# Gates of a recurrent branch: full 128-row matmuls with zero blocks, or two 64-row matmuls side by side

## The chip, the cores and the metric

One core of one Trainium2 chip runs the whole kernel as one launch. The time is device microseconds (us) of that core. TensorE (PE) multiplies matrices and writes to PSUM, ScalarE (ACT) evaluates functions, VectorE (DVE) does elementwise work, GpSimd (POOL) some small work, and SyncE (SP) issues the DMAs.

## The reference

An encoder trunk of two layers on 512 tokens of width 1024. In each layer one projection of the normalised input feeds four mixers, whose outputs are gated, projected, merged and added. The branch at stake is B, a recurrent unit on 384 channels in 6 blocks of 64, run forward and backward:

```python
xb = xc.reshape(b, s, B_BLOCKS, B_BLOCK_DIM)          # 6 blocks of 64
r = sigmoid(einsum("bsnc,ncd->bsnd", xb, w_r).reshape(b, s, w) + b_r)
i = sigmoid(einsum("bsnc,ncd->bsnd", xb, w_i).reshape(b, s, w) + b_i)
log_a = -B_C * r * softplus(-lam)
a = exp(log_a)
u = sqrt(-expm1(2.0 * log_a)) * (i * xc)
h = associative_scan(h[t] = a[t] * h[t-1] + u[t])     # per direction, the two are summed
```

Here xc is the output of a short depthwise convolution. The two gates r and i of a block are 64 x 64 matrices applied to that block's 64 channels.

## The kernel before, in words

Activations lie with channels on the 128 partitions and the 512 tokens along the free dimension. Every fp32 operand is split into a high and a low part of type fp32r, and a product is three matmuls, high x high, high x low and low x high (`mm3`, line 435). The low part is a subtraction on DVE, the high part a copy on ACT (`split`, line 427).

Three streams of work are generators: the dense stream (projections, gates, output), a side stream that runs the attention branches D, C and A one after another, and the recurrent branch (`side_B`, line 1290). `drive` (line 1854) asks them for their next steps and interleaves them. A planner (`Sched`, line 96) holds a clock for each engine and prices each instruction; it issues PE's instructions at once and holds those of the other engines back until they are due. Its price for a matmul of type fp32r with 256 or more columns goes by the columns alone (line 188), so 64 rows cost as much as 128. What comes out is one fixed order of instructions for each engine.

A stream tells through its yields what it waits for: `("c", n)` ends a step, `("w", label)` waits for another stream, `("n", k)` for free slots, and `self.at(..., S=1)` for operands and for that many free PSUM banks of pool S. Pool S has two banks (`BANKS`, line 46), and the scores of the attention branches use the same pool: D takes one bank at a time, C two. The recurrent branch is paced by its count of steps: between `B_FROM` and `B_TO` of the dense stream's cost in a layer it should make `B_STEPS` of them (line 54, used in `behind`, line 1902).

For each layer, `side_B` issues the DMAs of the gate weights into three zeroed tiles, one for each chunk of 128 channels, which is two blocks. Both blocks stand on the diagonal of a 128 x 128 matrix, one matrix for each direction and gate, and the other two quarters are zero. For each chunk it then computes the convolution on DVE, splits it into xh and xl, and for each direction and gate runs one trio of matmuls into one bank of pool S, followed by one tanh on ACT that reads the bank. Further ACT and DVE work and a scan on DVE follow. The result is handed over under the label yb, for which the dense stream waits (`split_y`, line 760) right behind the projection of a_v, which is 384 columns wide.

Branch C's scores already use halves of the rows. This is the form that they have (line 1431):

```python
for x, y in ((0, 0), (0, 1), (1, 0)):
    for c in range(2):
        r = slice(64 * c, 64 * c + 64)
        PE.matmul(Sb[c], (qh, ql)[x][r, s], (kh, kl)[y][r], start=(x == 0 and y == 0), stop=(x == 1))
```

The biases and other small parameters are loaded as rows, one per 128 channels, and turned once at the start, so that each becomes a column of the tile prm (`ROWS`, line 37; `load_params`, line 1739; `par`, line 1732).

Of the kernel before, what the change touches and what calls it, by code (L numbers as in the profile page):

```python
# [12 lines left out]
AF = mybir.ActivationFunctionType  # L13
# [3 lines left out]
P = 128  # L17
# [7 lines left out]
for _n, _s in IN_SPLITS:  # L25
# [8 lines left out]

K_C, K_A1, K_A23, K_RT, K_RN, K_QS, K_END = 0, 896, 1280, 1536, 2048, 2304, 2436

ROWS = {"b_gate": (0, 32), "conv_w": (64, 12), "conv_b": (88, 3), "lru_br": (94, 6), "lru_bi": (106, 6),
        "lru_lambda": (128, 6), "diff_subln": (140, 1), "mla_q_norm": (142, 2), "mla_kv_norm": (146, 1)}

P_QN, P_SUB, P_HSP, P_NSP, P_LAM = 0, 4, 6, 18, 30  # L40
# [10 lines left out]
SIDE_RESERVE = 9  # L51
LAYER_COST = 2670.0
PACE = ((80, 0), (940, 230), (1720, 430), (2290, 582))
B_FROM, B_TO, B_STEPS = 170, 560, 70
AHEAD = 0.1
AHEAD_OF = {"A": 0.7, "V": 0.7, "G": 0.7, "D": 100.0}
DELTA = {"s": 0.0, "d": 1.5, "w": 1.5, "b": 10.0}
# [306 lines left out]
class Trunk:  # L364
# [925 lines left out]
    def side_B(self, l):  # L1290
        nc, I = self.nc, self.I
        V, S = nc.vector, nc.scalar
        yield ("w", ((l, "hT"), 3))
        yield ("n", 3)
        raws = []
        for i in range(3):
            t = self.slot("lru")
            nc.gpsimd.memset(t, 0.0)
            v = t.rearrange("p (d w e) -> p d w e", d=2, w=2)
            for wi, wn in enumerate(("lru_wr", "lru_wi")):  # L1300
                src = I[wn][l].rearrange("d n c e -> n c d e")
                for o in range(2):
                    nc.sync.dma_start(v[64 * o:64 * o + 64, :, wi, 64 * o:64 * o + 64], src[2 * i + o])
            raws.append(t)
        yield ("w", (l, "bx"))
        for i in range(3):
            yield ("n", 9)
            wh, wl = self.slot("lruh", F32R), self.slot("lrul", F32R)
            self.split(wh, wl, raws[i])
            self.rel(raws[i])  # L1310
            bx = self.T.pop(f"bx{i}")
            xc = self.slot("xc")
            cw = lambda j: self.par("conv_w", l, 3 * j + i)
            V.tensor_scalar(xc, bx, cw(1), self.par("conv_b", l, i), op0=OP.mult, op1=OP.add)
            yield ("c", 0)
            V.scalar_tensor_tensor(xc[:, 1:], bx[:, :511], cw(0), xc[:, 1:], op0=OP.mult, op1=OP.add)
            yield ("c", 0)
            V.scalar_tensor_tensor(xc[:, :511], bx[:, 1:], cw(2), xc[:, :511], op0=OP.mult, op1=OP.add)
            yield ("c", 0)
            V.scalar_tensor_tensor(xc[:, :510], bx[:, 2:], cw(3), xc[:, :510], op0=OP.mult, op1=OP.add)  # L1320
            self.rel(bx)
            yield ("c", 0)
            xh, xl = self.slot("xch", F32R), self.slot("xcl", F32R)
            self.split(xh, xl, xc)
            yield ("c", 0)
            D = []
            for d in range(2):
                pr = []
                for wi, row in ((0, "lru_br"), (1, "lru_bi")):
                    yield self.at(wl, xl, S=1)  # L1330
                    B = self.ps("S")
                    c = slice((2 * d + wi) * P, (2 * d + wi) * P + P)
                    self.mm3(B, wh[:, c], wl[:, c], xh, xl, True, True)
                    t = self.slot("lg")
                    S.activation(t, B, AF.Tanh, scale=0.5, bias=self.par(row, l, 3 * d + i, self.prm_h))
                    pr.append(t)
                    yield ("c", 3)
                tr, ti = pr
                a = self.slot("la")
                k = 6 * l + 3 * d + i  # L1340
                hsp, nsp = self.der(P_HSP + k), self.der(P_NSP + k)

                S.activation(a, tr, AF.Exp, scale=nsp, bias=nsp)
                S.activation(tr, tr, AF.Tanh, scale=hsp, bias=hsp)
                yield ("c", 0)
                V.scalar_tensor_tensor(a, a, 1.0, tr, op0=OP.add, op1=OP.mult)
                V.tensor_scalar(a, a, -1.0, 1.0, op0=OP.mult, op1=OP.add)
                yield ("c", 0)
                V.scalar_tensor_tensor(ti, ti, 1.0, xc, op0=OP.add, op1=OP.mult)
                yield ("c", 0)  # L1350
                V.scalar_tensor_tensor(ti, a, 1.0, ti, op0=OP.add, op1=OP.mult)
                D.append((a, tr, ti))
                yield ("c", 0)
            self.rel(wh, wl, xh, xl, xc)
            for a, w, ti in D:
                S.activation(w, w, AF.Sqrt, scale=0.25, bias=self.tiny)
            for d, (a, w, ti) in enumerate(D):
                V.tensor_mul(ti, ti, w)
                yield ("c", 0)
                if d == 0:  # L1360
                    V.tensor_tensor_scan(w, a, ti, 0.0, op0=OP.mult, op1=OP.add)
                else:
                    V.tensor_tensor_scan(w[:, ::-1], a[:, ::-1], ti[:, ::-1], 0.0, op0=OP.mult, op1=OP.add)
                self.rel(a, ti)
                yield ("c", 0)
            if i == 0:
                yield ("w", (l, "ub"))
            u, w0, w1 = self.T.pop(f"ub{i}"), D[0][1], D[1][1]
            V.tensor_add(w0, w0, w1)
            yield ("c", 0)  # L1370
            V.tensor_mul(u, u, w0)
            self.rel(w0, w1)
            self.y_done("b", i, u, (l, "yb") if i == 2 else None)
            yield ("c", 0)
# [357 lines left out]
    def par(self, name, l, i, tile=None):  # L1732
        c = ROWS[name][0] + ROWS[name][1] * l + i
        return (self.prm if tile is None else tile)[:, c:c + 1]
# [4 lines left out]
    def load_params(self):  # L1739
        nc, I = self.nc, self.I  # L1740
        rows, lam = self.slot("rows"), self.slot("lam")
        nc.gpsimd.memset(rows[:, :256], 0.0)
        for name, (r, n) in ROWS.items():
            ap = I[name]
            c = P * (r // P)
            r, n = r % P, n * DEPTH
            nc.sync.dma_start(rows[r:r + n, c:c + P], bass.AP(tensor=ap.tensor, offset=ap.offset, ap=[[P, n], [1, P]]))
        v = lam.rearrange("p (i l c) -> p i l c", i=4, l=DEPTH)
        for i, n in enumerate(("diff_lam_q1", "diff_lam_k1", "diff_lam_q2", "diff_lam_k2")):
            s = I[n]  # L1750
            nc.sync.dma_start(v[:, i], bass.AP(tensor=s.tensor, offset=s.offset, ap=[[0, P], [64, DEPTH], [1, 64]]))
        self.rows = (rows, lam)

    def params(self):
# [8 lines left out]
        V.tensor_copy(self.prm, T[:, :256])  # L1763
        col = lambda n: self.prm[:, ROWS[n][0]:ROWS[n][0] + ROWS[n][1] * DEPTH]

# [220 lines left out]
```

## Time and profile before

| what | value |
|---|---|
| median of 3 runs | 1549.57 us (1548.51 to 1549.97) |
| the profiled execution's own time | 1549.14 us |
| its span, first to last instruction | 1547.4 us |
| busy PE / DVE / ACT / POOL | 1532.6 / 882.4 / 735.3 / 61.0 us |
| instructions | 21989 |
| mean granted TensorE clock | 0.996 |

Matmuls overlap: one lasts about 0.39 us in the records, and the next may start 0.23 us after it. So in a timeline the distance between two starts is what a matmul takes of PE. All instructions carry line 315, that of the planner's helper, so the tiles tell them apart: xch and xcl are the two parts of the convolution's output, lruh and lrul those of the gate weights, lg the gates, ck and cq the keys and queries of branch C, yb the branch's output.

### The profile page before, as it was taken

The page shows a single profiled execution, that of the slowest core. Times are in us where ns is not written, and L with a number is a line of the kernel's source. Part 1 is how long each engine was busy: PE and PEld are TensorE (multiplying, and loading weights), DVE is VectorE, ACT ScalarE, POOL GpSimd, SP SyncE. Part 2 cuts the span into 40 slices and gives each one's busy share as a digit, 9 for nine tenths or more (in the row PEclk, how much of TensorE's full clock was granted, in tenths as well). Part 3 has the DMA queues.
Part 4 walks back from the last instruction along what each step waited for, and adds up shares of the span by engine and source line. Part 5 has one row for each costly group of instructions (what it writes and reads, how often), then busy time and mean ns, then how long its engine had stood idle before and what let it go on. Part 6 is the DMA issues. An engine that isn't in the chain of part 4 may idle for free.

```text
span 1547.4 us, 21989 instructions
## 1 busy us (share of the span) xinstructions
PE 1532.6 (99%) x8024; PEld 1254.7 (81%) x8024; DVE 882.4 (57%) x1898; ACT 735.3 (48%) x1626; POOL 61.0 (4%) x254
## 2 busy tenths in 40 slices
PE   8999999999999999999999999999999999999998
PEld 8888888788887888888888878887787887788886
DVE  5698755446544453556658876544546446445553
ACT  5676653343444543443457765434435445334331
POOL 1300000000000100000020000000000001000000
PEclk9999999999999999999999999999999999999999
DMA  6422132223232324253252222232232223332621
GB/s 210 143 58 58 45 103 79 79 72 96 69 81 70 87 75 108 59 175 108 73 165 55 69 55 77 81 87 66 79 97 62 77 74 86 81 96 59 186 70 55
DMA packets 170884, 136.34 MB, mean 88 GB/s; under 512 B 25230, under 2 KB 158360, under 8 KB 170648
## 3 DMA queue, kind: packets, MB, share of 16 engines
q1 hardware_dynamic: 170776, 134.94, 31.3%
q8 instruction: 63, 1.03, 0.3%
q14 instruction: 45, 0.37, 0.1%
HBM read 129.45 MB, written 4.27 MB: 86 GB/s over the span
## 4 chain that ended last, share of the span: by engine, by line
PE 96%; DVE 1%; ACT 1%; DMA 0%; issue 0%; SPq 0%; DVEq 0%; ACTq 0%
PE ps L315 96%; DMA st<-in_w_in 0%; ACT lg L315 0%; DVE wl L315 0%; DVE lg L315 0%; DVE hTl L315 0%; ACT hTh L315 0%; ACT wh L315 0%; DVE rr L315 0%; SPq L315 0%; DVE rp L315 0%; ACT h L315 0%; ACT L315 0%; DVE x L315 0%; ACT la L315 0%
## 5 line engine op out<-in xcount | busy, mean ns | idle before, releaser
L315 PE MATMUL ps<-hTh,wh 128*128 128x512 f32 x1280 | 515.8, 403 | 1.1 <-DVE ud L315 1.1
L315 PE MATMUL ps<-hTl,wh 128*128 128x512 f32 x1280 | 499.7, 390 | 0.0
L315 PE MATMUL ps<-hTh,wl 128*128 128x512 f32 x1280 | 499.5, 390 | 0.0
L315 DVE TENSOR_TENSOR wl<-st,wh 128x512 fp32r<-128x512 f32 (+2 forms) x464 | 301.6, 666 | 272.0 <-ACT wh L315 271.1
L315 PEld LDWEIGHTS ps<-hTh,wh 128*128 128x128 f32 x1280 | 240.4, 188 | 62.8 <-issue 12.8
L315 ACT ACTIVATE wh<-st 128x512 fp32r<-128x512 f32 (+2 forms) x464 | 265.5, 606 | 42.2 <-DMA st<-in_w_in 35.9
L315 PEld LDWEIGHTS ps<-hTh,wl 128*128 128x128 f32 x1280 | 240.3, 188 | 52.2
L315 PEld LDWEIGHTS ps<-hTl,wh 128*128 128x128 f32 x1280 | 240.8, 188 | 44.5
L315 DVE CUSTOM_DVE_ANT_0 pC<-ps,cst 128x512 f32<-128x512 f32 x64 | 41.6, 689 | 81.5 <-PE ps L315 81.5
L315 PE MATMUL ps<-wh,hTh 128*128 128x416 f32 (+2 forms) x192 | 71.6, 373 | 0.6 <-ACT hTh L315 0.6
L315 PE MATMUL ps<-wl,hTh 128*128 128x416 f32 (+2 forms) x192 | 70.2, 365 | 1.7 <-DVE wl L315 1.6
L315 PE MATMUL ps<-wh,hTl 128*128 128x416 f32 (+2 forms) x192 | 69.9, 364 | 0.1
L315 ACT ACTIVATE pA<-pA,on 128x256 f32<-128x256 f32 x96 | 47.9, 501 | 38.1 <-DVE on L315 37.9
L315 ACT ACTIVATE pD<-ps,mx 128x512 f32<-128x512 f32 x48 | 33.0, 687 | 65.9 <-DVE mx L315 65.7
L315 ACT ACTIVATE pC<-pC,mx 128x512 f32<-128x512 f32 x64 | 45.8, 717 | 36.2 <-DVE mx L315 36.2
L315 DVE CUSTOM_DVE_ANT_0 pA<-ps,cst 128x256 f32<-128x256 f32 x96 | 36.0, 420 | 31.5 <-PE ps L315 31.4
L315 PE MATMUL ps<-wh,mh 128*128 128x512 f32 x128 | 50.0, 390 | 0.0
L315 PE MATMUL ps<-wh,ml 128*128 128x512 f32 x128 | 49.8, 389 | 0.0
L315 PE MATMUL ps<-wl,mh 128*128 128x512 f32 x128 | 49.8, 389 | 0.0
L315 ACT ACTIVATE wtC<-ps 128x512 f32<-128x512 f32 x32 | 19.1, 596 | 50.5 <-PE ps L315 50.5
L315 ACT ACTIVATE junk<-ps,rd 128x128 f32<-128x128 f32 x32 | 11.7, 365 | 63.8 <-DVE oC L315 63.1
L315 PEld LDWEIGHTS ps<-wl,hTh 128*128 128x128 f32 x192 | 36.6, 191 | 5.9 <-DVE wl L315 2.8
(390 smaller groups left out, 2207.8 us busy)
## 6 DMA issues: line engine op xcount, KB each, us to landing
st<-in_w_in SPq DMA_DIRECT2D x216, 256.0 KB
st<-in_w_in SPq DMA_DIRECT2D x240, 128.0 KB
st<-in_w_out SPq DMA_DIRECT2D x32, 256.0 KB
x<-in_x SPq DMA_DIRECT2D x16, 256.0 KB
st<-in_w_br_c SPq DMA_DIRECT2D x16, 256.0 KB
x<-x SPq DMA_DIRECT2D x16, 256.0 KB
st<-in_w_in SPq DMA_DIRECT2D x16, 208.0 KB
st<-in_w_in SPq DMA_DIRECT2D x16, 192.0 KB
```

Of the source, the lines that this page charges most:

```text
L315: op.fn(*op.a, **op.k)
```

## The change

The two gates of a block now stand side by side in the 128 columns of the stationary operand, and the two blocks of a chunk in the two halves of the rows. A group of six matmuls, each on 64 rows, gives both gates of both blocks for one direction, in two banks: bank o holds block o, its partitions 0 to 63 the first gate, 64 to 127 the second. Four tanh on 64 partitions each read them, and write the gates in the layout as before, so what follows is unchanged. The gate tiles are 256 columns wide, without zeros and without the memset. The biases of the two gates are loaded side by side in one row per block, so that one column holds both.

```diff
-B_FROM, B_TO, B_STEPS = 170, 560, 70
+B_FROM, B_TO, B_STEPS = 170, 560, 64
...
             t = self.slot("lru")
-            nc.gpsimd.memset(t, 0.0)
-            v = t.rearrange("p (d w e) -> p d w e", d=2, w=2)
+            v = t[:, :256].rearrange("p (d w e) -> p d w e", d=2, w=2)
...
-                    nc.sync.dma_start(v[64 * o:64 * o + 64, :, wi, 64 * o:64 * o + 64], src[2 * i + o])
+                    nc.sync.dma_start(v[64 * o:64 * o + 64, :, wi, :], src[2 * i + o])
...
-            self.split(wh, wl, raws[i])
+            self.split(wh[:, :256], wl[:, :256], raws[i][:, :256])
...
-                pr = []
-                for wi, row in ((0, "lru_br"), (1, "lru_bi")):
-                    yield self.at(wl, xl, S=1)
-                    B = self.ps("S")
-                    c = slice((2 * d + wi) * P, (2 * d + wi) * P + P)
-                    self.mm3(B, wh[:, c], wl[:, c], xh, xl, True, True)
-                    t = self.slot("lg")
-                    S.activation(t, B, AF.Tanh, scale=0.5, bias=self.par(row, l, 3 * d + i, self.prm_h))
-                    pr.append(t)
-                    yield ("c", 3)
-                tr, ti = pr
+                yield self.at(wl, xl, S=2)
+                B = [self.ps("S"), self.ps("S")]
+                c = slice(d * P, d * P + P)
+                for x, y in ((wh, xh), (wh, xl), (wl, xh)):
+                    for o in range(2):
+                        r = slice(64 * o, 64 * o + 64)
+                        self.PE.matmul(B[o], x[r, c], y[r], start=(x is wh and y is xh), stop=(x is wl))
+                tr, ti = self.slot("lg"), self.slot("lg")
+                for o in range(2):
+                    for g, t in enumerate((tr, ti)):
+                        r = slice(64 * g, 64 * g + 64)
+                        S.activation(t[64 * o:64 * o + 64], B[o][r], AF.Tanh, scale=0.5,
+                                     bias=self.par("lru_b", l, 6 * d + 2 * i + o, self.prm_h)[r])
+                yield ("c", 4)
...
+            if name == "lru_b":
+                for i, m in enumerate(("lru_br", "lru_bi")):
+                    ap = I[m]
+                    nc.sync.dma_start(rows[r:r + n, c + 64 * i:c + 64 * i + 64],
+                                      bass.AP(tensor=ap.tensor, offset=ap.offset, ap=[[64, n], [1, 64]]))
+                continue
```

## Rows read from the trace of the kernel before

**Rows 1.** Engine shares: busy us (share of the span) x instructions

```profile
PE 1532.6 (99%) x8024; PEld 1254.7 (81%) x8024; DVE 882.4 (57%) x1898; ACT 735.3 (48%) x1626; POOL 61.0 (4%) x254
```

**Rows 2.** The chain that ended last, by engine

```profile
PE 96%; DVE 1%; ACT 1%; DMA 0%; issue 0%; SPq 0%; DVEq 0%; ACTq 0%
```

**Rows 3.** Waits of PE: waited for, us in total, times, longest

```profile
PE ps L315 <- DVE h L315: 2.8, 3, 1.2
PE ps L315 <- DVE wl L315: 1.6, 2, 1.0
PE ps L315 <- DVE ud L315: 1.1, 1, 1.1
PE ps L315 <- DVE z L315: 1.1, 1, 1.1
PE ps L315 <- ACT hTh L315: 0.6, 1, 0.6
```

**Rows 4.** Timeline of PE, both gates of one direction: start, duration, instruction

```profile
77.73 0.39 PE L315 MATMUL ps<-xch,lruh 128*128 128x512 f32 x1
77.96 0.39 PE L315 MATMUL ps<-xcl,lruh 128*128 128x512 f32 x1
...
79.09 0.39 PE L315 MATMUL ps<-wh,hTh 128*128 128x512 f32 x1
```

**Rows 5.** Groups of instructions by form, PE: count, busy us, mean ns

```profile
L315 PE MATMUL ps<-xch,lruh 128*128 128x512 f32 x24 | 9.6, 402 | 0.0
```

**Rows 6.** Timeline of PE, the stretched trio

```profile
153.32 0.40 PE L315 MATMUL ps<-xch,lruh 128*128 128x512 f32 x1
153.75 0.50 PE L315 MATMUL ps<-xcl,lruh 128*128 128x512 f32 x1
154.09 0.39 PE L315 MATMUL ps<-xch,lrul 128*128 128x512 f32 x1
```

**Rows 7.** Timeline of PE, a group of branch C and its neighbours

```profile
299.52 0.39 PE L315 MATMUL ps<-hTh,wl 128*128 128x512 f32 x1
299.84 0.50 PE L315 MATMUL ps<-ck0h,cq0h 64*128 64x512 f32 x2
300.17 0.40 PE L315 MATMUL ps<-ck0l,cq0h 64*128 64x512 f32 x2
300.41 0.40 PE L315 MATMUL ps<-ck0h,cq0l 64*128 64x512 f32 x2
300.73 0.50 PE L315 MATMUL ps<-hTh,wh 128*128 128x512 f32 x1
301.07 0.40 PE L315 MATMUL ps<-hTl,wh 128*128 128x512 f32 x1
```

**Rows 8.** Groups of instructions by form, ACT

```profile
L315 ACT ACTIVATE lg<-ps,prmh 128x512 f32<-128x512 f32 x24 | 16.2, 682 | 6.1 <-PE ps L315 5.9
...
L315 ACT ACTIVATE lruh<-lru 128x512 fp32r<-128x512 f32 x6 | 3.7, 618 | 0.0
L315 ACT ACTIVATE ktd<-ps 64x512 f32<-64x512 f32 x6 | 3.6, 596 | 1.1 <-DVE ktl L315 1.0
```

**Rows 9.** Timeline of ACT, two tanh end to end

```profile
79.57 1.24 ACT L315 ACTIVATE lg<-ps,prmh 128x512 f32<-128x512 f32 x2
```

**Rows 10.** Busy time by stretch: busy us (x instructions), PEclk, DMA share, GB/s

```profile
80.00:175.00 95.00, 94.85 (x479) 76.84 (x478) 79.90 (x138) 67.72 (x127) 0.00 (x0) 1.00 0.22 56
840.00:935.00 95.00, 93.94 (x475) 76.37 (x474) 75.69 (x130) 67.87 (x123) 0.00 (x0) 1.00 0.23 59
```

**Rows 11.** Timeline of ACT, the tanh of the stretched trio

```profile
156.69 0.69 ACT L315 ACTIVATE lg<-ps,prmh 128x512 f32<-128x512 f32 x1
```

**Rows 12.** Timeline of PE, the last matmul of a_v in layer 0

```profile
193.75 0.33 PE L315 MATMUL ps<-wh,hTl 128*128 128x384 f32 x1
```

**Rows 13.** Instructions of the tile yb2l: duration min/median/max, first and last start

```profile
L315 DVE SCALAR_TENSOR_TENSOR yb2l<-ub,yb2h x2: 693/694/695, 183.7 to 945.9; 128x512 fp32r<-128x512 f32 x2
```

More of the change, by code (lines that the diff above doesn't have):

```diff
@@ L35 @@
 K_C, K_A1, K_A23, K_RT, K_RN, K_QS, K_END = 0, 896, 1280, 1536, 2048, 2304, 2436
-ROWS = {"b_gate": (0, 32), "conv_w": (64, 12), "conv_b": (88, 3), "lru_br": (94, 6), "lru_bi": (106, 6),
+ROWS = {"b_gate": (0, 32), "conv_w": (64, 12), "conv_b": (88, 3), "lru_b": (94, 12),
         "lru_lambda": (128, 6), "diff_subln": (140, 1), "mla_q_norm": (142, 2), "mla_kv_norm": (146, 1)}
@@ L1743, in load_params @@
         for name, (r, n) in ROWS.items():
-            ap = I[name]
             c = P * (r // P)
             r, n = r % P, n * DEPTH
+            if name == "lru_b":
[4 more added lines that the diff above has]
+                continue
+            ap = I[name]
             nc.sync.dma_start(rows[r:r + n, c:c + P], bass.AP(tensor=ap.tensor, offset=ap.offset, ap=[[P, n], [1, P]]))
```

## Prediction

> **What bounds the kernel now.** I read the engine shares first: TensorE (PE) is busy for 1532.6 of the 1547.4 us span, 99%, and no other engine passes 57% [rows 1]. The chain that ended last lies on PE for 96% [rows 2]. So a microsecond of matmul time taken off PE should be a microsecond off the end, unless PE starts to wait. What PE waits for now is the third view: five groups, 2.8 + 1.6 + 1.1 + 1.1 + 0.6 = 7.2 us in all [rows 3], and none of them is a wait for a PSUM bank or for the recurrent branch. The reader is to see in these three that the order of matmuls which the planner writes leaves almost nothing between them, and that the price of a matmul is therefore not its listed duration (0.39 us, which overlaps the next one) but the distance from its start to the next start.
>
> **What the recurrent branch costs PE today.** For each of 2 layers, 3 chunks of 128 channels and 2 directions, two gates are computed with three full 128-row matmuls of 512 columns each: 72 matmuls, 24 of each of three kinds [rows 5]. Two such trios, the two gates of one direction, stand end to end from 77.73 to 79.09, where the next full matmul starts: 1.36 us for six, 0.227 each [rows 4]. 72 x 0.227 = 16.3 us. One trio is stretched, 153.32 to 153.75 to 154.09, the matmul that reads xcl starting late [rows 6]: (0.43 + 0.34) - 2 x 0.227 = 0.3 us more. I don't count that as a gain, because a late operand can meet a new order as well.
>
> **What it will cost.** The new group is six matmuls for both gates of a direction: for each of the three products, one on rows 0 to 63 and one on rows 64 to 127, into two banks. Branch C computes its scores in exactly this shape (64 rows, 128 stationary columns, 512 moving columns, two banks, the same order of products), so the trace of before has the price [rows 7]. The last full matmul ahead starts at 299.52; three pairs start at 299.84, 300.17 and 300.41 (each row is a pair, x2, and the two of a pair start together); full matmuls follow at 300.73 and 301.07. Without the six, the two full neighbours take 2 x 0.227 = 0.454. With them it is 301.07 - 299.52 = 1.55. So a group costs 1.55 - 0.454 = 1.096 us. Its parts: three pair steps of about 0.227 would be 0.68; the rest, 0.42, is 0.09 on the way in (0.32 for 0.227), 0.10 behind the first pair, 0.09 behind the last and 0.11 on the first full matmul after (0.34 for 0.227).
>
> The Trainium skill (TensorEngine Tiling (Array Packing), Theoretical Speedup) gives up to twice the speed for a contraction of 64 or less. By that a group would cost half of six full matmuls. The same page (Tiling Modes, Key Properties) says that a change of tiling mode drains TensorE, and the 0.42 us at the edges of C's group agree with that one. The sum below goes by the measured group.
>
> Twelve groups cost 12 x 1.096 = 13.15 us. The saving on PE is 16.34 - 13.15 = 3.2 us, 0.27 per group. A lower bound for a group is 0.68 us (no edges, saving 8.2); an upper one is six full steps with the edges, 1.36 + 0.20 = 1.56 (a loss of 2.4), for the case that the halves don't overlap. I take 1.096 because that is a row of the same shape in the same surroundings. The edges can't be shared between groups: a group takes both banks of the pool S, so two of them can't stand side by side.
>
> **The other edits.** (a) Tanh: 24 instructions of 128 x 512 become 48 of 64 rows x 512. A copy of 64 rows out of PSUM takes 596 ns, the tanh of 128 rows 682, so the number of rows is not what sets it [rows 8]; two tanh end to end took 1.24 us for 0.67 each, so a further one costs ACT about 0.57 [rows 9]. 24 x 0.57 = +13.7 us on ACT. In the stretches where the branch runs ACT is busy 67.7 of 95 us and 67.9 of 95, DVE 79.9 and 75.7 [rows 10]; ACT goes to about 74.5, 78%. That is beside PE's work and costs nothing as long as it stays there. If the cover goes, one tanh is 0.57 us. (b) The splits of the gate weights run on 256 columns instead of 512: 618 ns on ACT [rows 8] falls by something between 0 and half, at most 0.3 x 6 = 1.9 us, on ACT, and alike on DVE; nothing on PE. (c) Six memsets leave GpSimd, which is busy 4% [rows 1]: zero. (d) DMAs: the twelve weight loads per layer stay twelve with as many bytes, only packed; the two bias loads at the start stay two, at the same place of the queue. Between nothing and a few tenths either way; I take zero. (e) Pacing: the branch now hands control back 63 times instead of 69 per layer and B_STEPS goes from 70 to 64, so its pace is kept. The planner prices six of these matmuls as six full ones, 1.3 us, as it did before, so its clock doesn't move; PE will be 0.27 us earlier than planned per group. (f) The new wait: a group needs both S banks free, where a trio needed one. Behind it on PE stands whatever the planner put there, and D's next score, which wants an S bank as well.
>
> **Sum.** The profiled execution took 1549.14 us (span 1547.4); 1549.14 - 3.2 = 1545.9. The median of the runs, 1549.57, lies 0.43 above, so the forecast in its terms is 1549.57 - 3.2 = 1546.3 after rounding down the tenth that the stretched trio may give.
>
> **The rivals.**
>
> 1. The order is shuffled and gives something back. Every decision of the planner after the first group rests on clocks that shift, so the waits of PE and the number of row-mode changes come out anew. Two of the present waits, wl 1.6 and ud 1.1 [rows 3], are of the kind that such a shuffle makes or removes. Three new ones of this size (0.5 to 1.1 each) would give back 1 to 3 us: 1547.3 to 1549.5, say 1548.2. If it takes the present ones away instead, 2.7 us more are won: 1543.6. For it: nothing holds the order fixed. Against a large effect: PE is fed at 99% in all stretches.
>
> 2. Slower: the banks come back late. In the old order a trio issued at 153.32 had its tanh only at 156.69 to 157.38 [rows 6, 11], so ACT held that bank 3 us behind the matmuls while the other one served D. Now four tanh, 2.3 us, stand on two banks, and D's next score has neither. PE takes its instructions in order, so if ACT is one tanh later than the planner thinks, PE stands still 0.57 us per group, 6.8 in all: 1546.3 + 6.8 = 1553.1. It decides from 0.27 us per group, where the saving is eaten. The Trainium skill warns of this (TensorEngine Tiling (Array Packing), PSUM Bottleneck): tiling doesn't speed up what empties PSUM. For it: ACT's work per gate doubles, in the busiest stretches. Against: PE has no wait on a bank today [rows 3], ACT is idle for a quarter of these stretches [rows 10], and C's groups, which take both banks in the same way, put no wait in that list. A second form has the branch late as a whole: its last part yb2l ends at 183.7 + 0.7 = 184.4 [rows 13], and the dense stream must have it once the last a_v matmul has gone, and that one starts at 193.75 [rows 12]. The slack is 9.4 us, and 12 further tanh of one layer are 6.8, so this doesn't bite unless the waits for both banks add 2.7.
>
> 3. The halves don't overlap, so that the change doesn't do what it says: a loss of 2.4 us by the upper bound, 1552.0. The pairs of C speak against it [rows 7].
>
> 4. The edges vanish. If the weight loads of the halves hide behind the matmuls ahead, a group costs three steps, 3 x 0.227 = 0.68 us, and the twelve save 12 x (1.36 - 0.68) = 8.2: 1541.4. Against it stands that C's group pays its edges on both sides [rows 7]. This is what the page's factor of two would come to here.
>
> **How the numbers follow.** What a measurement of this kernel can tell from no change is about 0.2%, 3.1 us: faster means under 1546.5, slower over 1552.7. My forecast, 1546.3, stands on that edge, so its own spread (1545.0 to 1548.0) is cut in two. Chances: forecast 0.52 (0.34 faster, 0.18 same); shuffle that gains 0.10 (faster); shuffle that gives back 0.24 (0.20 same, 0.04 slower); banks late or the branch late 0.09 (slower); no overlap 0.02 (0.01 same, 0.01 slower); no edges 0.03 (faster). Faster 0.47, same 0.39, slower 0.14. The range takes in the gaining shuffle below and the loss up to the middle of rival 2: 1543.4 to 1551.0.
>
> **What the new profile would show.** Rows of 64 x 512 matmuls from xch, in pairs, three steps of about 0.33, 0.24 and 0.32 us; PE busy down by about 3 us; 48 tanh of 0.68 us; yb2l ending before the last a_v matmul. Wrong would be: PE waits of more than 0.27 us per group that end with a tanh on ACT (rival 2), single steps of 0.22 us inside a pair (rival 3), or a group far from 1.10 us. If the group costs 1.10 and the time still falls by less than 3 us, the list of PE's waits must have grown by the difference.

## The result, and the profile after

The changed kernel takes 1559.42 us (median of 6 runs, 1557.1 to 1560.2) against 1549.37 for the kernel before (6 runs): ratio 1.0064, interval 1.0053 to 1.0074. It is slower by 10 us where 1546.3 was forecast, and outside the range of 1543.4 to 1551.0. The span of the profiled execution goes from 1547.4 to 1557.4.

The rows of the page that answer to [rows 1, 2]:

```profile
PE 1535.0 (99%) x8024; PEld 1251.4 (80%) x8024; DVE 881.9 (57%) x1898; ACT 752.4 (48%) x1650; POOL 58.1 (4%) x248
...
PE 89%; ACT 6%; DVE 3%; issue 1%; DMA 1%; SPq 0%; DVEq 0%; ACTq 0%
```

ACT has 17.1 us more work, and the chain, 96% on PE before, now leaves it for ACT and DVE. The shares of busy time alone would not have told: PE is at 99% in both. Nearly all of ACT's added work is the tanh itself, 32.8 us where [rows 8] have 16.2:

```profile
L315 ACT ACTIVATE lg<-ps,prmh 64x512 f32<-64x512 f32 x48 | 32.8, 683 | 12.1 <-PE ps L315 11.2
```

The price of the new group came out as predicted. Timeline of PE after (start, duration, instruction), the first group of the second chunk:

```profile
122.89 0.39 PE L315 MATMUL ps<-hTh,wl 128*128 128x512 f32 x1
123.21 0.50 PE L315 MATMUL ps<-xch,lruh 64*128 64x512 f32 x2
123.55 0.40 PE L315 MATMUL ps<-xcl,lruh 64*128 64x512 f32 x2
123.78 0.40 PE L315 MATMUL ps<-xch,lrul 64*128 64x512 f32 x2
124.11 0.50 PE L315 MATMUL ps<-hTh,wh 128*128 128x512 f32 x1
124.44 0.40 PE L315 MATMUL ps<-hTl,wh 128*128 128x512 f32 x1
```

124.44 - 122.89 = 1.55 us, the figure of branch C's group [rows 7]. One group of the twelve is stretched: its neighbours start at 910.62 and 912.79, 2.17 us apart, 0.6 more. What was lost stands in the list of PE's waits (us in total, times, longest), the answer to [rows 3]:

```profile
PE ps L315 <- DVE h L315: 3.2, 3, 1.1
PE ps L315 <- DVE pD L315: 3.0, 2, 2.2
PE ps L315 <- DVE wl L315: 3.0, 2, 2.4
PE ps L315 <- ACT wh L315: 1.9, 1, 1.9
PE ps L315 <- DVE ktl L315: 1.6, 1, 1.6
PE ps L315 <- DVE z L315: 1.1, 1, 1.1
PE ps L315 <- DVE cq0l L315: 0.3, 1, 0.3
PE ps L315 <- DVE qtl L315: 0.2, 1, 0.2
PE ps L315 <- ACT lg L315: 0.2, 1, 0.2
```

They sum to 14.5 us, against 7.2 before: +7.3. Only the last row, 0.2 us, is a wait for the recurrent branch's own tanh. The rows for h and z, 4.3 us together, stood in the list before with 3.9. What grew are waits that end with a weight split (wl, wh), a softmax of branch D (pD) or a key of D (ktl), which have nothing to do with the change. The chain of waits shows how the longest of them got late. Its pieces in order of time (start, duration, what), ending at that stop (the pieces of 1.28 us without a tile are loads of ACT's function tables, of which there are 21 before and after):

```profile
176.05 1.28 ACT L315
177.35 0.72 ACT lg L315
178.09 1.28 ACT L315
179.38 0.78 ACT pD L315 x2
180.18 1.28 ACT L315
181.48 0.73 ACT lg L315
182.23 0.70 DVE lg L315
182.96 1.24 DVE lg L315
184.22 0.70 DVE lg L315
184.98 0.69 issue
185.67 0.69 DVE rp L315
186.39 0.57 DVE wl L315
187.00 604.99 PE ps L315 x3205
```

ACT finishes the branch's second square root at 182.2. DVE has to run its products and the scan (the row named issue is one of these products) before it comes to the weight split wl, whose turn in the written order is at 186.39, and PE stands still until 187.00. The stop has a further cost, the clock behind it. Timeline of PE, and below it busy time by stretch (PEclk is the granted clock):

```profile
184.06 0.33 PE L315 MATMUL ps<-wh,hTl 128*128 128x384 f32 x1
184.23 0.34 PE L315 MATMUL ps<-wh,hTh 128*128 128x384 f32 x1
187.00 0.69 PE L315 MATMUL ps<-wl,hTh 128*128 128x384 f32 x1 [2.43 <-DVE wl L315]
187.49 0.52 PE L315 MATMUL ps<-wh,hTl 128*128 128x384 f32 x1
187.81 0.52 PE L315 MATMUL ps<-wh,hTh 128*128 128x384 f32 x1
```

```profile
187.00:189.80 2.80, 2.80 (x9) 2.80 (x10) 2.61 (x4) 1.42 (x5) 0.00 (x0) 0.50 0.36 94
896.50:899.80 3.30, 3.30 (x11) 2.73 (x11) 3.24 (x6) 0.89 (x2) 0.00 (x0) 0.50 0.00 0
958.00:961.20 3.20, 3.20 (x13) 3.10 (x13) 2.85 (x4) 2.62 (x7) 0.00 (x0) 0.50 0.34 80
```

Before the stop the matmuls of 384 columns step by 0.17 us, after it by 0.32, and the granted clock is 0.50, 1.2 GHz. The same follows two other long stops, at 894 and 954 us; the kernel before has no such stretch between 20 and 1540 us. These 9.3 us at half clock lose half, 4.7. So the sum is +7.3 of waits, +4.7 of clock, and a rest of 10.0 - 12.0 = -2.0, in which the predicted -3.2 of matmul time lies, and the 0.6 of the stretched group against the 0.3 of the stretched trio before [rows 6]; about 1 us of it I can't place.

### The profile page after: what moved, and what is told of

The parts are those of the page before. It is cut to its first block, busy times and chain, and to the rows that moved or that the text cites. A ratio compares the mean times of both kernels' runs of the same rounds, so it can differ in the third digit from the quotient of the medians.

```text
span 1557.4 us, 22020 instructions
## 1 busy us (share of the span) xinstructions
PE 1535.0 (99%) x8024; PEld 1251.4 (80%) x8024; DVE 881.9 (57%) x1898; ACT 752.4 (48%) x1650; POOL 58.1 (4%) x248
## 4 chain that ended last, share of the span: by engine, by line
PE 89%; ACT 6%; DVE 3%; issue 1%; DMA 1%; SPq 0%; DVEq 0%; ACTq 0%
PE ps L315 89%; ACT lg L315 3%; ACT L315 1%; ACT wh L315 1%; DVE lg L315 1%; DMA st<-in_w_in 1%; ACT la L315 1%; DVE rp L315 0%; DVE wl L315 0%; ACT pD L315 0%; SPq L315 0%; ACT qth L315 0%; DVE rr L315 0%; ACT cv L315 0%; ACT ptD L315 0%
## 5 line engine op out<-in xcount | busy, mean ns | idle before, releaser
L315 PEld LDWEIGHTS ps<-wh,hTh 128*128 128x128 f32 x192 | 37.6, 196 | 8.2 <-ACT wh L315 2.6
```

The costliest lines, as they stand in the source:

```text
L315: op.fn(*op.a, **op.k)
```

## The experiments

Theory A: the 24 further tanh make ACT late against an order that is fixed beforehand; DVE stands behind ACT, PE behind DVE. Theory B: the new order is bad in itself, whatever ACT does. "The order is kept" means that the planner decides as in the other kernel and only what is issued differs. All ratios are to the kernel before, run beside it.

**1. The order of the changed kernel, short tanh.**

```diff
+                        if o == g:
+                            fn = lambda *a, t=t, B=B[o], c=bias, **k: self.tc.nc.scalar.activation(t, B, AF.Tanh, scale=0.5, bias=c)
+                        else:
+                            fn = lambda x, y, f, **k: self.tc.nc.scalar.activation(x[:, :1], y[:, :1], f, **k)
...
```

> The order of the changed kernel on every engine is kept as it is, but where the planner thinks of four tanh per group, two are 128-row tanh of a whole bank and two read a single column. The gates are therefore not what the reference wants; only the time is read. ScalarE's tanh work falls from about 48 x 0.71 = 34 us to about the 24 x 0.6 of the kernel before. Theory A (ScalarE's added work makes ScalarE, then VectorE behind it, late against the written order, and TensorE stands still at 184, 149, 894 and 954 us, each long stop also costing 1.7 us of half clock): the long waits shrink to under 0.5 us, the dips of the clock go, and the time falls by about 7 + 5 = 10 us or more, to 1546 to 1550. Theory B (the written order itself is the bad part, whatever ScalarE's load): the waits stay and the time stays at 1556 to 1560. Both wrong in part: 1551 to 1555.

1545.06 us, ratio 0.9978 (0.9968 to 0.9987). The same matmuls in the same order are faster than the kernel before, by 3.4 us (2.0 to 5.0 by the interval), as the prediction had it for PE alone. ACT still issues 48 tanh per execution there, so it is their time and not their number that counts. The waits of that run sum to 8.1 us, and its mean granted clock is 0.998 where the changed kernel has 0.993. Three rows that answer to the ones above:

```profile
...
PE ps L315 <- DVE wl L315: 1.7, 3, 0.8
PE ps L315 <- DVE pD L315: 1.2, 1, 1.2
...
PE ps L315 <- ACT wh L315: 0.5, 1, 0.5
```

**2. The order of the kernel before, each tanh in two halves.**

```diff
+                    def fn(t, B, f, scale, bias):
+                        for r in (slice(0, 64), slice(64, 128)):
+                            self.tc.nc.scalar.activation(t[r], B[r], f, scale=scale, bias=bias[r])
...
```

> The order of the kernel before is kept on every engine, with its full-row matmuls and single banks; each of the 24 tanh is issued as two of 64 rows, of which the planner knows nothing. So ScalarE gets the added work alone, 24 x about 0.71 = 17 us. Theory A: TensorE begins to wait as in the changed kernel, 1554 to 1563. Theory B: the order of before has slack for it, 1549 to 1551.

1564.86 us, ratio 1.0104 (1.0089 to 1.0119): 18 us of ACT work (753.4 us busy for 735.3) cost 16.4 us. The old matmuls and the old order, with the new tanh alone, are slower than the whole change. Its two longest stops end the same way, with D's result ud, which DVE writes behind the branch's scan. Here PE also waits for the branch's tanh to empty a bank, four times, which is rival 2 as it was written:

```profile
PE ps L315 <- DVE ud L315: 6.8, 2, 3.8
...
PE ps L315 <- ACT lg L1337: 2.6, 4, 1.1
```

**3. The kernel before with the new pace.**

```diff
-B_FROM, B_TO, B_STEPS = 170, 560, 70
+B_FROM, B_TO, B_STEPS = 170, 560, 64
```

> The kernel before with B_STEPS 64 in place of 70, nothing else: an equal amount of work in another order of the steps. Theory A: an order shuffled without added work on ScalarE moves the time by less than 3 us, 1547 to 1552. Theory B (any shuffle of the order of the recurrent branch can cost this much): it may move by 5 us or more.

1547.42 us, ratio 0.9993 (0.9984 to 1.0003). This shuffle alone did no harm.

**4. The right price for the tanh.** The planner prices a tanh at 0.57; in the trace four of 64 rows take 2.81 us (runs 13 and 14 below show the row), one lasts 0.68, so each further one takes (2.81 - 0.68) / 3 = 0.71.

```diff
             fn = a[2]
+            if fn == AF.Tanh and a[0].shape[0] == 64:
+                c = 0.71
```

> The changed kernel with one line more in the planner's price list: a tanh on 64 rows costs 0.71 us, as the trace shows, where it was priced at 0.57. Same instructions, other order. Theory A in its narrow form (the planner doesn't know of the added 0.14 us per tanh, 0.55 per group, and writes weight splits too late behind the branch's work): the time comes back to 1546 to 1551. If the lateness comes mostly from ScalarE and VectorE instructions of all kinds that are priced too low, and the added load only removes the slack, this helps little: 1553 to 1560.

1548.63 us, ratio 1.0000 (0.9990 to 1.0009). This looked like the cure, so I varied it.

**5 to 8. The old pace, two other prices, and a second price mended.**

> The changed kernel with B_STEPS 70 as before, so the pacing edit alone is undone; the price of the tanh stays at 0.57. If the planner's ignorance of ScalarE's time is the cause, this is only another order with the same ignorance: 1553 to 1563, with stops of TensorE of over 1.5 us. If the pacing edit, or the luck of that one order, was the cause, it falls to 1551 or less.

> The changed kernel with a 64-row tanh priced at 0.43 us, as far below the 0.57 of the changed kernel as that lies below the measured 0.71. If the time follows the price, it is slower than the changed kernel by another 5 to 12 us, 1564 to 1572. If the gain of the right price was one lucky order among many, it lies anywhere between 1546 and 1563.

> The changed kernel with two prices mended: 0.71 us for a 64-row tanh, and 0.183 us (1.10 / 6) for each 64-row matmul of 512 columns, those of branch C too, in place of 0.216. Same instructions. If what is left of the gap to the short-tanh run (1545.1) is that TensorE runs ahead of the planner's clock, this gives 1544.5 to 1547.5. If the gap is ScalarE's load itself, which no price removes, it stays at 1547 to 1550.

> The changed kernel with a 64-row tanh priced at 0.85 us, 0.14 above what it takes. If lateness against the plan is what costs, a price above the truth costs nothing or gains a little: 1545.5 to 1549.5. If only the exact price gave a good order by luck: 1551 or more.

| run | us | ratio (interval) |
|---|---|---|
| B_STEPS 70 | 1558.16 | 1.0064 (1.0046 to 1.0082) |
| tanh priced 0.43 | 1559.22 | 1.0075 (1.0056 to 1.0093) |
| 0.71, and pairs of matmuls priced too | 1559.75 | 1.0077 (1.0061 to 1.0093) |
| tanh priced 0.85 | 1563.31 | 1.0092 (1.0074 to 1.0110) |

```diff
-B_FROM, B_TO, B_STEPS = 170, 560, 64
+B_FROM, B_TO, B_STEPS = 170, 560, 70          # run 5
...
+            if fn == AF.Tanh and a[0].shape[0] == 64:
+                c = 0.43                          # run 6; 0.71 in run 7, 0.85 in run 8
...
+            if a[1].dtype == F32R and a[1].shape[0] == 64 and n == 512:
+                return 0.183                      # run 7
```

The pace is not the cause. But the time doesn't follow the price: 0.43, 0.57, 0.71 and 0.85 give 1559, 1559, 1549 and 1563. Theory A in its narrow form, that one wrong price is what is wrong, falls; run 4 is one good order among bad ones. A new order also changes how often ACT changes its function table. Loads of a table in runs 4, 7 and 8 (count, busy us, mean ns):

```profile
L317 ACT ACT_TABLE_LOAD x21 | 26.9, 1283 | 1.1 <-PEq L1983 0.7
L319 ACT ACT_TABLE_LOAD x25 | 32.1, 1283 | 1.2 <-PEq L1985 0.7
L317 ACT ACT_TABLE_LOAD x27 | 34.6, 1283 | 1.2 <-PEq L1983 0.7
```

So run 8 gives ACT 7.7 us more than run 4 to do, beside the tanh. That is not the whole reason: the changed kernel has 21 too and is slow, and run 3 has 27 and is not. In the run priced at 0.85 the branch is done late: its last part, yb2l, begins at 216.4 us in layer 0, and at 186.9 in the changed kernel. Timeline of PE there, from the last matmul ahead of the stops:

```profile
200.97 0.40 PE L317 MATMUL ps<-cTh,uql 128*128 128x512 f32 x1
204.55 0.63 PE L317 MATMUL ps<-ident,pD 128*128 128x128 f32 x4 [3.18 <-DVE pD L317]
207.36 1.11 PE L317 MATMUL ps<-ident,pD 128*128 128x128 f32 x4 [2.18 <-ACT ptD L317]
208.12 0.78 PE L317 MATMUL ps<-hTh,wh 128*128 128x512 f32 x1
```

No dense matmul stands between the last of a_v (197.72) and 208.12; PE has only branch D's work, and stops twice. By the code the dense stream is waiting there for the label yb, the second form of rival 2. That reading is argued from the code; the rows show the stops.

**9. The order of the run priced at 0.85, short tanh** (the edits of runs 1 and 8 together).

> The order of the run with the tanh priced at 0.85 us (1563.3) is kept, and as in the first experiment only two of four tanh per group do their work, the other two read one column; the gates are not the reference's. Theory L (ScalarE's added load decides, whatever the order): it falls to 1545 to 1550, as the order of the changed kernel did. Theory O (orders differ by luck, and this one is bad in itself, since the dense stream is held until the branch is done): it stays over 1555.

1559.04 us, ratio 1.0070 (1.0053 to 1.0087). The time stays over 1555, as theory O has it: of 14.8 us, 4.3 go with the tanh and 10.5 stay. But the two theories aren't cleanly parted by it. This order has 27 table loads, which stay when the tanh are short, so ACT is busy for 747.8 us here and for 740.3 in run 1. How much of the 10.5 us comes from that load and how much from the places of the instructions was not tested.

**10. Less other work on ACT.** In the changed kernel, two copies per chunk go to GpSimd:

```diff
-            self.split(wh[:, :256], wl[:, :256], raws[i][:, :256])
+            self.nc.gpsimd.tensor_copy(wh[:, :256], raws[i][:, :256])
+            V.tensor_sub(wl[:, :256], raws[i][:, :256], wh[:, :256].bitcast(F32))
...
-            self.split(xh, xl, xc)
+            self.nc.gpsimd.tensor_copy(xh, xc)
+            V.tensor_sub(xl, xc, xh.bitcast(F32))
```

> The changed kernel with two of the branch's copies, the high parts of the gate weights and of the convolution's output, moved from ScalarE to GpSimd: 6 x 0.41 + 6 x 0.63 = 6.2 us less on ScalarE, of the 17 added. GpSimd's price in the planner for wide work is raised to about 1.1 us. Theory L: a third of the loss comes back, 1553 to 1557, if GpSimd's copies are hidden. Theory O: another order, anywhere from 1547 to 1563. If GpSimd is slow or slows VectorE, it is slower than the changed kernel.

1553.28 us, ratio 1.0031 (1.0018 to 1.0045): in the stated band of theory L, but with another order, so it can't be told from luck.

**11 and 12. The branch's result needed later**, in the changed kernel and in the one before.

```diff
-B_FROM, B_TO, B_STEPS = 170, 560, 64          # run 11; run 12 keeps its 70 steps
+B_FROM, B_TO, B_STEPS = 170, 656, 64
...
+        cqk(2)
+        pair("c_g", 1, silu("c1"), "c_g", 2, silu("c2"), 2)
         split_y("b")
...
         drop_y("b")
-        cqk(2)
-        pair("c_g", 1, silu("c1"), "c_g", 2, silu("c2"), 2)
```

> The changed kernel with the place where the dense stream needs the branch's result moved back by 96 of its units (about 22 us of matmuls: the third pair of branch C and two gates go first), and B_TO from 560 to 656, so that the same ScalarE work is spread over a longer stretch. Theory L, in the form that it is the density of ScalarE's and VectorE's work in that stretch that counts: the stops of TensorE shrink and the gain on TensorE shows, 1545 to 1549.5. If the load costs wherever it lies: 1555 to 1562.

> The kernel before with the same two moves (the result needed 96 units later, B_TO 656). Both theories: its ScalarE load fits already, so 1546 to 1551; it is the control for the run above, whose gain over this one should be the 3.2 us of TensorE if spreading is the whole cure.

1560.06 (1.0074, 1.0059 to 1.0089) and 1553.39 (1.0029, 1.0018 to 1.0040). In this order spreading the work was no cure, and the move itself cost 4.9 us in the kernel before.

**13 and 14. Doses in a fixed order.** The bias left out of the four tanh, so that the gates lack it; and only one direction's tanh halved in the order of before.

```diff
+                        fn = lambda x, y, f, scale, bias: self.tc.nc.scalar.activation(x, y, f, scale=scale)      # run 13
...
+                    def fn(t, B, f, scale, bias, halves=(d == 0)):                                                # run 14
+                        for r in (slice(0, 64), slice(64, 128)) if halves else (slice(0, 128),):
+                            self.tc.nc.scalar.activation(t[r], B[r], f, scale=scale, bias=bias[r])
...
```

> The order of the changed kernel is kept on every engine, and each of the four tanh runs on its 64 rows and all 512 columns, but without the bias operand, so the gates lack their biases. A tanh without a bias column steps on by about 0.50 us in the trace, one of 64 rows with a bias by 0.71. If the bias is what sets the 0.71, ScalarE loses 48 x 0.2 = 10 us of work, and if ScalarE's time is the cause in this order, more than half of the loss comes back: 1546 to 1552. If the 64 rows set the step, it stays 0.71 and the time stays near 1559.

> The order of the kernel before is kept; only the 12 tanh of the forward direction are issued as two of 64 rows, the 12 of the other direction stay whole. The full dose cost 16.4 us (1564.9 against 1548.5) for 17 us of ScalarE work. If every us of ScalarE's time lands in the end because the chain through VectorE is always the last, half of it: 1556 to 1558. If there is slack that the first half uses up, 1549 to 1553.

1550.33 (1.0013, 1.0004 to 1.0023) and 1554.64 (1.0036, 1.0020 to 1.0052). Four tanh take 2.45 us without a bias and 2.81 with it, on ACT, in run 13 and in the changed kernel:

```profile
90.80 2.45 ACT L1339 ACTIVATE lg<-ps 64x512 f32<-64x512 f32 x4 [0.48 <-PE ps L315]
```

```profile
91.48 2.81 ACT L315 ACTIVATE lg<-ps,prmh 64x512 f32<-64x512 f32 x4 [0.49 <-PE ps L315]
```

That is 0.09 less for each of 48, 4.3 us of ACT time. Against the kernel before that ran beside each, the changed kernel is 10.1 us slower, run 13 1.4 slower and run 1 3.4 faster: so these 4.3 us bring back 8.6 of 13.5. In the order of before the first half of the load costs 5.7, the second 10.6. Both times the last microseconds of load cost most.

**15. The good order, short tanh** (the edits of runs 1 and 4 together).

> The order of the run with the tanh priced at 0.71 us (1548.6) is kept, and two of four tanh per group read one column only, so the gates are not the reference's. If that order hides ScalarE's added work wholly, it stays at 1547 to 1549. If it still pays for a part, as its waits of 2.8 us on weight splits suggest, it falls to 1543 to 1546, the bound that TensorE's own gain sets (1545.1 in the order of the changed kernel).

1546.42 us, ratio 0.9985 (0.9976 to 0.9995). Even that order pays about 2.3 us for the tanh.

**16 to 18. A version that keeps the gain?** First the price 0.71 with three copies per chunk on GpSimd, priced at 0.61; then the same copies with the order of run 4 kept, and with the order of before kept. The third copy, of the branch's result, is scaled by 0.5, and on GpSimd it is another instruction than the two plain ones (the edit of runs 17 and 18; run 16 calls GpSimd directly):

```diff
-        self.copy(hi, src, scale)
...
+            fn = (lambda x, y, f, **k: G.tensor_copy(x, y)) if scale is None else \
+                (lambda x, y, f, scale: G.tensor_scalar(x, y, scale, None, op0=OP.mult))
+            self.clk.call("A", "activation", fn, (hi, src, AF.Copy), {} if scale is None else dict(scale=scale))
...
```

> A version meant to keep TensorE's gain: the changed kernel with the 64-row tanh priced at 0.71, and three of the branch's copies per chunk (high parts of gate weights, of the convolution's output and of the branch's result) moved from ScalarE to GpSimd, where the 128 x 512 copy took 0.62 us; the planner's price for it is 0.61. ScalarE loses 10 of the 17 us added. If ScalarE's time is the cause, 1544.5 to 1548.5, faster than both. If the order rules, anywhere from 1545 to 1560.

> The order of the run with the tanh priced at 0.71 us (1548.6) is kept for every instruction, but the branch's 18 copies (high parts of gate weights, of the convolution's output and of the result) are issued on GpSimd in place of ScalarE; the planner doesn't know. ScalarE loses 6 x (0.41 + 0.63 + 0.63) = 10 us. With the same order the short tanh gave 1546.4, so ScalarE's time still costs 2.2 us there: if that is all that is left, 1546 to 1548, faster than the kernel before by 0.05 to 0.15%. If the copies on GpSimd (0.62 us, and a hand-over more) come later than on ScalarE for VectorE, which stands behind them, 1549 to 1552.

> The kernel before with the same 18 copies issued on GpSimd in the same order: the control that tells what relieving ScalarE does where there is no added tanh. The first half of the added work cost 5.8 us in this order, so ScalarE has no slack on that side; taking 11 us off should give back what waits are left for it, at most the 1.6 + 1.1 us for wl and ud: 1545.5 to 1548.5. Nothing or a loss if those waits belong to VectorE alone: 1548 to 1551.

1554.48 (1.0039, 1.0024 to 1.0054), 1551.65 (1.0017, 1.0008 to 1.0026) and 1550.91 (1.0013, 1.0004 to 1.0022). In the two kept orders ACT is busy 7.1 us less than in run 4 (17 of the 18 copies went) and 10.2 less than before, and the time is longer by 2.8 and 2.2 us. The plain copies mostly take no longer than on ACT, as the row of run 10 shows (duration min/median/max in ns). The scaled ones do: 1.8 us for 0.63, in run 18 and in the kernel before. In run 18 DVE, which writes the low part behind the copy, waits 5.5 us in all for the six scaled copies; the longest of these rows (us in total, times, longest) stands last:

```profile
L315 POOL CAST xch<-xc x6: 617/618/1881, 64.0 to 921.0; 128x512 fp32r<-128x512 f32 x6
L432 POOL TENSOR_SCALAR yb0h<-ub x2: 1792/1832/1871, 102.4 to 870.3; 128x512 fp32r<-128x512 f32 x2
L315 ACT ACTIVATE yb0h<-ub x2: 633/634/634, 101.8 to 869.8; 128x512 fp32r<-128x512 f32 x2
DVE yb2l L315 <- POOL yb2h L432: 2.3, 2, 1.4
```

So these runs don't show what relieving ACT alone is worth: the slower copies act against it, and with the plain copies alone no kept order was run. No version that computes all of the reference is faster than the kernel before by more than its interval.

## Why the prediction was wrong

- **PE's own cost.** Right. The group cost 1.10 us as worked out, and run 1, in which nothing but the tanh is short, is 3.4 us faster than before where 3.2 was forecast.
- **The tanh, step (a).** Here it failed, twice. The size: "a further one costs ACT about 0.57" was read from a 128-row pair [rows 9]; the 64-row ones step by 0.71, and ACT's busy time rose by 17.1 us, not 13.7 less the smaller splits. The sentence that decided: "That is beside PE's work and costs nothing as long as it stays there." It rested on ACT being busy for only three quarters of the stretch [rows 10]. Run 2 put that load alone into the old order: +16.4 us. A mean share of 75% was no cover in these two written orders: as the chain shows for the longest stop, late work on ACT delays the branch's DVE work, and DVE delays a weight split that PE needs at once. In the order of run 4 the same tanh cost only 2.3 us (run 15), so the price is one of the load and the order together.
- **Rival 2** named the right cause, ACT later than the planner thinks, at the wrong place. It had PE waiting for a bank of pool S; that wait is 0.2 us in the changed kernel (2.6 in run 2). The price, 6.8 us by rival 2, was 12: the waits alone are +7.3, and the fall of the clock behind them, 4.7, stood nowhere in the prediction. The prediction's last sign, that the list of PE's waits would have grown by the difference, asked for 13 us; the list grew by 7.3, and most of the rest is in the clock. The chance of this rival, 0.09, was far too low.
- **Its second form**, the branch late as a whole, was set aside for 9.4 us of slack, counted to the last a_v matmul. PE reads yb later than that: in the kernel before the first matmul on it starts at 208.15, behind 14 us of the branch's first output gates and other work, so the slack on the chip was larger. In the changed kernel the last part, yb2l, begins at 186.9 in layer 0, before the last a_v matmul (198.54), but at 976.0 in layer 1, behind it (969.54), as the row shows that answers to [rows 13]. There the first matmul on yb starts at 983.60, and no wait of PE names yb. In the orders of runs 8 and 9 it may decide, by the reading of the code above.

```profile
L315 DVE SCALAR_TENSOR_TENSOR yb2l<-ub,yb2h x2: 674/680/687, 186.9 to 976.0; 128x512 fp32r<-128x512 f32 x2
```

- **Rival 1**, the shuffle, was sized at 1 to 3 us from PE's present waits. The seven orders of the changed kernel's own instructions (the change itself, runs 4 to 8 and 11) gave 1548.6 to 1563.3. So an order is worth up to 15 us with the load on ACT. Without it run 3 moved by 1 us and run 12 by 5, but runs 1, 15 and 9, three orders with short tanh, lie between 1545.1 and 1559.0, 14 us apart, where run 9 has more table loads. The size given to this rival was too small by far.
- **The rule of the Trainium skill** (TensorEngine Tiling (Array Packing), PSUM Bottleneck), that tiling doesn't speed up what empties PSUM, pointed the right way: ACT's tanh work on the banks went from 16.2 us of busy time [rows 8] to 32.8, while the matmuls' cost, by their steps, fell by 3.2. It was given too little weight.

What stays open: why the order of run 4 is good where those of the change itself and of runs 5 to 8 are not. Neither the price that led to it nor the number of table loads is the reason by itself.

## What to carry to other kernels

Work moved off a full engine must be charged to the engine that takes it up, at its step in the new shape, and a mean share of 75% need not be a cover in a kernel whose order is fixed beforehand: put the added load alone into the old order (run 2) before trusting it. Where a planner's order decides, one run of a changed price proves nothing; vary it, or keep the order and change what is issued, and look at what else the new order changed. A long stop of TensorE costs more than its length when the clock falls behind it, as it did after three stops here.

## What the runs showed of the hardware that I had not expected

- ScalarE's tanh of 64 x 512 from PSUM with a bias column takes 683 ns and steps by 0.71 us; of 128 rows it takes 682 and stepped by 0.57 [rows 8, 9]. Without the bias, 64 rows take 594 ns and step by 0.62, (2.45 - 0.59) / 3. So halving the rows saved nothing and lost some overlap; what sets the step of the 64-row form was not settled.
- Six 64-row matmuls in three pairs cost 1.10 us in place of 1.36, a factor of 1.24, not 2: of the 0.68 us that three pairs could save, 0.42 go at the edges of the group and behind its first pair.
- GpSimd's plain cast of 128 x 512 from f32 to fp32r took 0.62 us in the median of run 10 (once 1.88), as ScalarE's copy does [rows 8]. With a factor of 0.5 it took 1.5 to 1.9 us in runs 16 to 18, where ScalarE takes 0.63.
